# A hybrid RWKV-7 / S5 / RG-LRU layer on one core: gate banks read at another priority, GroupNorm squares one tick sooner, S5 poles fetched at the start, SBUF pools opened in another order

## The chip, the core and the metric

The kernel runs on one core of a Trainium2 chip. A core has a matrix engine (TensorE, in the profile PE, with its weight loads as PEld), a vector engine (VectorE, DVE), an engine for activation functions (ScalarE, ACT), a general engine (GpSimd, POOL) and a queue that issues transfers (SyncE, SP). Each works through its own list of instructions in order, and waits for the others by semaphores. Data lie in SBUF (128 partitions), sums of matmuls in PSUM (8 banks of 128 x 512 float32 here), all else in HBM.

The metric is the device time of one execution in microseconds (us). Before the change it was 1810.94 us, the median of three runs (1809.5 to 1812.85).

## The reference

One layer over a sequence of 2048 positions of width 1024, all float32, then a norm. `linear_binop` joins two steps of a linear recurrence; the helpers that are left out are plain.

```python
def hybrid_layer(h, p_i, norm_g, w_in, ..., w_out, ple_w, ple_norm_g, ple_gate_w):
    zin = rmsnorm(h, norm_g) @ w_in                       # 1024 -> 4224
    z_rw, g_rw, u_s5, g_s5, x_lru, g_lru = jnp.split(zin, SPLITS, axis=-1)
    y_rw = rwkv7_group(z_rw, g_rw, ...)                   # 8 heads of 64
    y_s5 = s5_group(u_s5, g_s5, ...)                      # 32 groups, 64 complex states each
    y_lru = rglru_group(x_lru, g_lru, ...)                # 8 blocks of 64
    h = h + jnp.concatenate([y_rw, y_s5, y_lru], axis=-1) @ w_out
    e = rmsnorm(p_i @ ple_w, ple_norm_g)
    return h + e * jax.nn.sigmoid(h @ ple_gate_w)

# RWKV-7, one step and what follows it
    S = S * d - (S @ kk) b^T + v k^T ;  y = S @ r
    y = (y - mean(y)) * rsqrt(var(y) + RWKV_GN_EPS) * ln_w + ln_b     # GroupNorm by head
    y = (y + sum(r * k * r_k) * v) * silu(gate)

# RG-LRU
    r = sigmoid(xc @ wa + ba) ;  i = sigmoid(xc @ wx + bx)            # blocks of 64
    log_a = -LRU_C * r * softplus(-lam) ;  a = exp(log_a)
    h_t = a_t * h_(t-1) + sqrt(-expm1(2 * log_a)) * (i * xc) ;  y = h * silu(gate)

# S5
    lam = complex(a_re, a_im) ;  lam_bar = exp(lam * dt)              # the poles
    x_t = lam_bar * x_(t-1) + b_bar u ;  y = real(c x) + d u ; then gelu, a gated 512 x 512 product, silu(gate)
```

The outputs of the three groups are gated by their own columns of the input projection.

## The kernel before

**Precision.** A large product is made of three matmuls at float32r: both operands are split into a high and a low part (`whi`, `wlo`, `xh`, `xl`; the high part is a cast on ScalarE, the low part a subtraction on VectorE), and high x high, low x high and high x low are added up in one PSUM bank. So one 128 x 128 weight block and 512 positions cost the three matmuls of L345, L346 and L347 in the input projection, or L949, L950 and L951 in the helper `mm3`.

**First stage: input projection with the RWKV-7 and RG-LRU mixers (to about 1145 us).** The sequence is taken in two halves of 1024, each in two blocks of 512 (`TB`). `fills` yields the input projection column block by column block, and what is done with each: `z` for RWKV, `g` its gates, `l` for RG-LRU, `s` for S5, whose inputs go to HBM for later. Beside the fills run three stages of RWKV, each a generator, over 16 units (two pairs of heads x 256 positions): `front_stage` makes the decayed keys and their products (`kx`, `gr`, `mt`, `bk`), `solve_stage` inverts the triangular systems (`ms`, `xs`, `stmp`, `tm`), `chain_stage` carries the state over four steps of 64 positions, and then norms and gates.

The order on TensorE is written out by hand (`manual_schedule`): a clock of ticks; in each tick the fills issue 10 or 8.8 matmuls' worth (`CHUNK_MM`), and then each stage that is due issues one piece. `yield n` in a stage puts its next piece n ticks later. On the other engines, and on the SP queue, a list scheduler orders the instructions when the kernel is built, by priority (program order less an offset) and by a model of when each is ready. `tc.high_priority` gives the offset: the chain `PR_C` = 100, the solve 50, front and fills 0; `PR_B` = 100 is used for single instructions. After the tick loop TensorE is ordered by the scheduler too.

*RG-LRU gates.* The two gate products of a block are made while a later column block is projected, after its third and fifth group of matmuls (`K_LATE`): `decay_gate` (L686) and `input_gate` (L706) each write a bank of the ring of three that the fills use as well (`ps_mm`). The bank is free for a projection again when ScalarE has read it: twice for the decay gate (`lr` by Abs, `la` by Relu), once for the input gate (`li` by Tanh). The tiles `lr`, `la`, `lth`, `li`, `z`, `xc`, `us`, `g` are buffers of one ring of eight (`tf`).

*GroupNorm of the chain.* A chain's step has three pieces; after the last one of the last step it yields, then ScalarE squares the outputs (`rst` from the bank `ps_y`), it yields again, and L633 sums the squares over the heads into the bank `ps_late`. ScalarE reads that by Ln, and takes Exp for the root. `ps_late` is a single bank, also written by the solve of the next unit (L548, L562). VectorE multiplies, adds the bonus `bon`, multiplies by the gate `g2`, and two transfers store `rst` in HBM (`Yd`).

**Second stage: S5 beside a part of the output projection.** `o1a` makes the product of w_out with the RWKV and RG-LRU outputs, 16 tiles of 128 positions. It needs a tile of `Yd`, loaded as `yr` and split into `yh` and `yl` (`split_y`), and eight rows of w_out, each loaded into a staging buffer `st` and split into `woh` and `wol` (`split_rows`). `yr` and `st` share a ring of three buffers (pool `hq`). The first tile is multiplied row by row, so that it can start with the first row. In the same stretch VectorE works out the S5 parameters from the poles: `a_re` and `a_im` come in by four transfers, two transposes on TensorE (L1035, L1036) turn them, and `ar` and `ai` are copied out.

**Last stages.** The S5 output gate with the rest of w_out, then the per-layer embedding, its gate and the final norm.

**SBUF.** Pools on the right side are stacked from the right edge of SBUF inwards in the order in which they are opened; within a pool, the tag that is asked for first lies at the lowest address, the farthest from the edge. The pools of the first stage on that side, in their order: `rz` (13 KB a partition: `zk`, `zr`, `zl`, `wab`, `pt`, `sp`, `sn`), `rf` (16: the ring `tf`), `re` (8: `bon`, `g2`, `rst`), `rl` (44: `kb`, `gr`, `dl`, `kx`, `tm`, `uv`), `rv` (4: `zv`), `rw` (28: `tp` 12, `bk`, `ms`, small ones, `ep`, `inv`, `mt`, `xs`, `stmp`). They are closed together, and the next stage's pools are stacked from the same edge: `hq` (12: `yr`, `st`, `ht`), `gwp` (16), `wq` (16: `yl`, `yh`), `wpb` (40: five rows of w_out), `wpa` (24: the first three rows). With `reuse_waits="tile"` a new tile waits for the last uses of just those old tiles whose addresses it covers.

Of the kernel before, what the change touches and what calls it, by code (L numbers as in the profile page):

```python
# [17 lines left out]
P = 128  # L18
# [27 lines left out]
def hymba_layer(ctx: ExitStack, tc: tile.TileContext, x, p, norm_g, w_in,  # L46
# [55 lines left out]
    def act(out, in_, func, scale=1.0, bias=0.0):  # L102
        A.activation(out=out, in_=in_, func=func, scale=scale, bias=bias)  # L103
# [17 lines left out]


    rws, xws = ExitStack(), ExitStack()
    rz = rws.enter_context(tc.tile_pool(name="rz", bufs=1, side="right", reuse_waits="tile"))
    rf = rws.enter_context(tc.tile_pool(name="rf", bufs=1, side="right", reuse_waits="tile"))
    re = rws.enter_context(tc.tile_pool(name="re", bufs=1, side="right", reuse_waits="tile"))
    rl = rws.enter_context(tc.tile_pool(name="rl", bufs=1, side="right", reuse_waits="tile"))
    rv = rws.enter_context(tc.tile_pool(name="rv", bufs=1, side="right", reuse_waits="tile"))
    rw = rws.enter_context(tc.tile_pool(name="rw", bufs=1, side="right", reuse_waits="tile"))
    POOL = {"tf": rf, "zk": rz, "zr": rz, "zv": rv, "bon": re, "g2": re, "tc": re}  # L130
    POOL.update((tag, rl) for tag in ("kx", "gr", "tm", "kb", "uv", "dl"))
    POOL.update((tag, rz) for tag in ("pt", "sn", "sp"))
# [167 lines left out]
    V.memset(lru_h, 0.0)  # L300
    s_carry = const.tile([P, 4, 64], F32, name="s_carry")
    V.memset(s_carry, 0.0)


    def lru_rates():
# [263 lines left out]
    def rwkv_chain(pair, half, q, q_, gd):  # L569
# [15 lines left out]
        for st in range(NS):  # L585
# [37 lines left out]
            for c in (st, st + NS):  # L623
                for h, hs in enumerate(heads):
                    T.matmul(out=psy[hs, c * C:(c + 1) * C], lhsT=uv[:, c, h], rhs=gr[:, c, h], start=False, stop=True,
                             tile_position=(0, 64 * h), skip_group_check=True)
            yield 1
        chained.append(0)
        rst = wt("rst")
        act(rst, psy, AF.Square)  # L630
# [48 lines left out]
    def lru(ct, half, xn, b, wg, wab, xc):  # L679
        g2 = gate2(tmp_f("g2"), (yield from inproj(xn, wg, b)))  # L680

        keep = []

        def decay_gate():
            psr = pmm()
            T.matmul(out=psr, lhsT=wab[:, 0], rhs=xc, start=True, stop=True)  # L686
            r_ = tmp_f("lr")
            act(r_, psr, AF.Abs, scale=0.5, bias=dcol(o_ba, ct))
            act(r_, r_, AF.Tanh)
            a = tmp_f("la")  # L690
            act(a, psr, AF.Relu, scale=-1.0, bias=dcol(o_nba, ct))
            act(a, a, AF.Exp, scale=-1.0)

            stt(r_, r_, 1.0, a, ALU.add, ALU.mult)
            th = tmp_f("lth")
            act(th, r_, AF.Tanh, scale=dcol(o_sp, ct))
            act(a, r_, AF.Exp, scale=dcol(o_sm, ct))
            act(r_, a, AF.Square)
            stt(th, r_, 1.0, th, ALU.add, ALU.mult)
            act(th, th, AF.Sqrt, scale=0.25)  # L700
            keep.append((r_, a, th))

        def input_gate():
            r_, a, th = keep[0]
            psi = pmm()
            T.matmul(out=psi, lhsT=wab[:, 1], rhs=xc, start=True, stop=True)  # L706
            ti = tmp_f("li")
            act(ti, psi, AF.Tanh, scale=0.5, bias=dcol(o_bx, ct))
            stt(ti, ti, 1.0, xc, ALU.add, ALU.mult)
            mul(ti, ti, th)  # L710
            h = r_
            V.tensor_tensor_scan(out=h, data0=a, data1=ti, initial=lru_h[:, ct:ct + 1], op0=ALU.mult, op1=ALU.add)
            V.tensor_copy(out=lru_h[:, ct:ct + 1], in_=h[:, TB - 1:TB])
            mul(h, h, g2)
            spill_y(h, Yd, 4 + ct, half * HALF + b * TB)

        late.extend((decay_gate, input_gate))
# [32 lines left out]
    def fills(half, xt, w, prev):  # L750
# [39 lines left out]
        yield from beside(lora(wl, zl, 0, xn), second, 1)  # L790
        yield from beside(rwkv_in(0, 0, zd[0], xn, 0, wk), second, 1)
        yield from second
        yield from lora(wl, zl, 1, xn)
        more()
        yield from rwkv_in(0, 0, zd[0], xn, 1, wk)
        if half == 0:
            lru_rates()

        def both(f, *a):
# [161 lines left out]

    s5c, ow = ExitStack(), ExitStack()
    hq = ctx.enter_context(tc.tile_pool(name="hq", bufs=1, side="right", reuse_waits="tile"))
    gwp = ctx.enter_context(tc.tile_pool(name="gwp", bufs=1, side="right", reuse_waits="tile"))
    wq = ctx.enter_context(tc.tile_pool(name="wq", bufs=1, side="right", reuse_waits="tile"))
    wpb = ow.enter_context(tc.tile_pool(name="wpb", bufs=1, side="right", reuse_waits="tile"))
    wpa = ow.enter_context(tc.tile_pool(name="wpa", bufs=1, side="right", reuse_waits="tile"))
    sc = s5c.enter_context(tc.tile_pool(name="s5c", bufs=1, side="left", reuse_waits="tile"))
# [26 lines left out]
        if i + 2 < NT:  # L995
            o1a_load(i + 2)

    NG = 32
    st32 = sc.tile([NG, 2, P], F32, name="st32")
    for i, src in enumerate((s5_a_re, s5_a_im)):  # L1000
        for h in range(2):
            nc.sync.dma_start(out=st32[:, i, 64 * h:64 * h + 64], in_=src[0])
    first_y = o1a_y(0)
    woh, wol = split_rows(wpa, w_out[0], (0, 1, 2), "wo", stage_q)
    for rows_, more in zip((woh, wol), split_rows(wpb, w_out[0], (3, 8, 9, 10, 11), "wo", stage_q)):
# [10 lines left out]
                o1a(i)  # L1016


    ar = sc.tile([P, NG], F32, name="ar")
    ai = sc.tile([P, NG], F32, name="ai")  # L1020
    al = sc.tile([P, NG], F32, name="al")
    thp = sc.tile([P, NG], F32, name="thp")
    rho = sc.tile([P, NG], F32, name="rho")
# [7 lines left out]
    pid = sc.tile([P, T5, NG], F32, name="pid")  # L1031
    tmps = [sc.tile([P, NG], F32, name=f"stm{i}") for i in range(8)]
    t0_, t1_, t2_, t3_, t4_, t5_, t6_, t7_ = tmps
    ps = pprep()
    T.transpose(out=ps[:, 0:NG], in_=st32[:, 0], identity=ident[0:NG, 0:NG])  # L1035
    T.transpose(out=ps[:, NG:2 * NG], in_=st32[:, 1], identity=ident[0:NG, 0:NG])  # L1036
    V.tensor_copy(out=ar, in_=ps[:, 0:NG])
    V.tensor_copy(out=ai, in_=ps[:, NG:2 * NG])
    nc.sync.dma_start(out=t0_, in_=s5_log_dt.broadcast_to([P, NG]))
    act(t0_, t0_, AF.Exp)  # L1040
    mul(al, ar, t0_)
# [400 lines left out]
```

## Time and profile before

| what | value |
|---|---|
| time, median of 3 runs | 1810.94 us (1809.5 to 1812.85) |
| the profiled execution's own time | 1812.73 us |
| its span, first to last instruction | 1810.8 us |
| mean granted TensorE clock | 0.984 |
| TensorE busy | 1730.4 us (96%) |
| VectorE, ScalarE busy | 1238.9 us (68%), 940.0 us (52%) |
| transfers, mean | 131 GB/s |

The profile gives for each engine what it did, how long, and, where it sat idle before an instruction, what ended that wait, in the form "idle us <- engine, tile, line". Lines are those of the kernel before. Ends of matmuls are modelled, so the pace of TensorE is read from start to start: 0.23 us for a matmul of 128 x 512. The granted clock is the share of its full rate that TensorE was given in a stretch.

### The profile page before, as it was taken

The numbers are of one execution on the slowest core, as the hardware profiler recorded it, in microseconds if no ns is written. First come the engines' busy times: TensorE is split into PE (matmuls) and PEld (weight loads), VectorE is DVE, ScalarE is ACT, GpSimd is POOL, SyncE is SP. The second block draws the span as 40 slices with busy tenths as digits, with TensorE's granted clock in tenths as the row PEclk, the third lists the DMA queues.
The fourth block names the chain that finished last, engine by engine and source line by source line (L and its number), as shares of the span: only waits on it lengthen the run. The fifth ranks groups of instructions, "written<-read, shape, count | busy, mean of one in ns | idle before, by whom it ended". The sixth has DMA issues, their size and how long they took to land. (4 is left out here: it accounts for less than half of the span.)

```text
span 1810.8 us, 30089 instructions
## 1 busy us (share of the span) xinstructions
PE 1730.4 (96%) x11212; PEld 1330.8 (73%) x11212; DVE 1238.9 (68%) x3121; ACT 940.0 (52%) x1792; POOL 43.8 (2%) x105
## 2 busy tenths in 40 slices
PE   5999899989998999999998999799999999999997
PEld 4877677767776777677766667588888778888886
DVE  6268877778897338877777875787866685555554
ACT  5346745575777433745557466475763452222222
POOL 1000000000000000000000000000000000000000
PEclk9999999999999999999999999899999999999999
DMA  5664435433444353234323232733324893222220
GB/s 194 213 202 138 152 108 170 161 104 118 148 134 137 117 178 143 87 106 138 131 82 96 72 96 81 208 123 109 119 89 142 221 310 125 85 104 100 83 68 35
DMA packets 198779, 236.61 MB, mean 131 GB/s; under 512 B 60309, under 2 KB 149738, under 8 KB 198634
## 3 DMA queue, kind: packets, MB, share of 16 engines
q1 hardware_dynamic: 198634, 234.70, 40.3%
q8 instruction: 88, 1.44, 0.3%
q14 instruction: 57, 0.47, 0.1%
HBM read 139.03 MB, written 94.44 MB: 129 GB/s over the span
## 5 line engine op out<-in xcount | busy, mean ns | idle before, releaser
L345 PE MATMUL ps_mm<-xh,whi 128*128 128x512 f32 x1056 | 466.0, 441 | 5.2 <-ACT la L103 5.2
L347 PE MATMUL ps_mm<-xl,whi 128*128 128x512 f32 x1056 | 417.4, 395 | 0.0
L346 PE MATMUL ps_mm<-xh,wlo 128*128 128x512 f32 x1056 | 417.0, 395 | 0.0
L345 PEld LDWEIGHTS ps_mm<-xh,whi 128*128 128x128 f32 x1056 | 200.5, 190 | 83.3 <-issue 32.3
L346 PEld LDWEIGHTS ps_mm<-xh,wlo 128*128 128x128 f32 x1056 | 201.3, 191 | 46.6 <-issue 13.9
L347 PEld LDWEIGHTS ps_mm<-xl,whi 128*128 128x128 f32 x1056 | 200.5, 190 | 45.6
L82 DVE TENSOR_TENSOR xs<-xs,stmp 128x60 f32<-128x60 f32 (+24 forms) x496 | 103.1, 208 | 12.7
L82 DVE TENSOR_TENSOR stmp<-xs,ms 128x60 f32<-128x60 f32 (+24 forms) x496 | 103.4, 209 | 12.1
L949 PE MATMUL ps_mm<-woh,yh 128*128 128x512 f32 x256 | 102.8, 402 | 3.8 <-ACT yh L103 3.8
L950 PE MATMUL ps_mm<-woh,yl 128*128 128x512 f32 x256 | 103.1, 403 | 1.0 <-DVE yl L100 1.0
L951 PE MATMUL ps_mm<-wol,yh 128*128 128x512 f32 x256 | 101.7, 397 | 0.0
L951 PE MATMUL ps_mm<-pgl,hh 128*128 128x512 f32 x256 | 101.1, 395 | 0.3 <-DVE pgl L82 0.3
L950 PE MATMUL ps_mm<-pgh,hl 128*128 128x512 f32 x256 | 100.9, 394 | 0.0
L949 PE MATMUL ps_mm<-pgh,hh 128*128 128x512 f32 x256 | 100.8, 394 | 0.0
L103 ACT ACT_TABLE_LOAD x75 | 96.2, 1283 | 1.3
L100 DVE SCALAR_TENSOR_TENSOR z<-ps_mm,pc,z 128x511 f32<-128x511 f32 x48 | 35.7, 743 | 77.9 <-ACT z L103 77.6
L103 ACT ACTIVATE ftg<-ps_mm 128x512 f32<-128x512 f32 x32 | 19.1, 598 | 134.4 <-PE ps_mm L951 134.4
L100 DVE SCALAR_TENSOR_TENSOR e<-ftg,e 128x1024 f32<-128x1024 f32 x16 | 19.6, 1225 | 77.2 <-ACT ftg L103 77.2
L103 ACT ACTIVATE z<-ps_mm,dc 128x512 f32<-128x512 f32 x48 | 32.9, 686 | 73.9 <-PE ps_mm L347 73.7
L103 ACT ACTIVATE uv<-ps_chain 64x128 f32<-64x128 f32 x64 | 17.4, 272 | 80.6 <-DVE uv L95 60.2
L949 PEld LDWEIGHTS ps_mm<-woh,yh 128*128 128x128 f32 x256 | 48.5, 190 | 14.3 <-ACT yh L103 4.3
L595 ACT COPY sn<-uv 64x128 f32<-64x128 f32 x96 | 28.4, 296 | 58.3 <-DVE uv L82 56.8
(332 smaller groups left out, 3493.0 us busy)
## 6 DMA issues: line engine op xcount, KB each, us to landing
wraw<-in_w_in SPq DMA_DIRECT2D x66, 256.0 KB
Wd<-whi SPq DMA_DIRECT2D x33, 512.0 KB
Wd<-wlo SPq DMA_DIRECT2D x33, 512.0 KB
wlo<-Wd SPq DMA_DIRECT2D x33, 512.0 KB
whi<-Wd SPq DMA_DIRECT2D x33, 512.0 KB
zd<-z SPq DMA_DIRECT2D x48, 256.0 KB
yr<-Yd SPq DMA_DIRECT2D x16, 512.0 KB
Hd<-ht SPq DMA_DIRECT2D x16, 512.0 KB
```

The source lines that it names most:

```text
L82: V.tensor_tensor(out=out, in0=a, in1=b, op=op)
L100: V.scalar_tensor_tensor(out=out, in0=a, scalar=s, in1=b, op0=op0, op1=op1)
L103: A.activation(out=out, in_=in_, func=func, scale=scale, bias=bias)
L345: T.matmul(out=ps, lhsT=hi[:, k], rhs=xh, start=(k == 0), stop=False)
L346: T.matmul(out=ps, lhsT=lo[:, k], rhs=xh, start=False, stop=False)
L347: T.matmul(out=ps, lhsT=hi[:, k], rhs=xl, start=False, stop=(k == KD - 1))
L595: A.copy(out=sn[hs], in_=uv[hs, cs, h])
L949: T.matmul(out=ps, lhsT=a_h[:, k], rhs=b_h[k][:, ns], start=(ends[0] and k == 0), stop=False)
L950: T.matmul(out=ps, lhsT=a_l[:, k], rhs=b_h[k][:, ns], start=False, stop=False)
L951: T.matmul(out=ps, lhsT=a_h[:, k], rhs=b_l[k][:, ns], start=False, stop=(ends[1] and k == nk - 1))
```

## The change

1. In `decay_gate` the two reads of the bank (Abs, Relu) stand together ahead of the Tanh, at the priority offset `PR_B`; in `input_gate` the read by Tanh has that offset too.
2. The chain doesn't yield after the last piece of its last step, so that the squares belong to that tick, and L633 to the next one.
3. The poles are fetched in the first half, after the second block of x has been made ready, into a buffer of the ring `tp`; two transposes and one copy bring them into a constant tile after the first RWKV columns. The second stage no longer loads, transposes or copies them.
4. The first stage's pools on the right side are opened in the order `rw`, `rf`, `rz`, `rv`, `rl`, `re`; in the second stage `wq` comes before `gwp`.

```diff
+    rw = rws.enter_context(tc.tile_pool(name="rw", bufs=1, side="right", reuse_waits="tile"))
+    rf = rws.enter_context(tc.tile_pool(name="rf", bufs=1, side="right", reuse_waits="tile"))
     rz = rws.enter_context(tc.tile_pool(name="rz", bufs=1, side="right", reuse_waits="tile"))
-    rf = rws.enter_context(tc.tile_pool(name="rf", bufs=1, side="right", reuse_waits="tile"))
+    rv = rws.enter_context(tc.tile_pool(name="rv", bufs=1, side="right", reuse_waits="tile"))
+    rl = rws.enter_context(tc.tile_pool(name="rl", bufs=1, side="right", reuse_waits="tile"))
     re = rws.enter_context(tc.tile_pool(name="re", bufs=1, side="right", reuse_waits="tile"))
-    rl = rws.enter_context(tc.tile_pool(name="rl", bufs=1, side="right", reuse_waits="tile"))
-    rv = rws.enter_context(tc.tile_pool(name="rv", bufs=1, side="right", reuse_waits="tile"))
-    rw = rws.enter_context(tc.tile_pool(name="rw", bufs=1, side="right", reuse_waits="tile"))
...
+    NG = 32
+    poles = const.tile([P, 2, NG], F32, name="poles")
+    ar, ai = poles[:, 0], poles[:, 1]
+
+    def pole_rows():
+        t = tmp_p("st32")[0:NG, 0:2 * P].rearrange("g (i p) -> g i p", i=2)
+        for i, src in enumerate((s5_a_re, s5_a_im)):
+            for h in range(2):
+                nc.sync.dma_start(out=t[:, i, 64 * h:64 * h + 64], in_=src[0])
+        return t
+
+    def pole_columns(t):
+        ps = pprep()
+        for i in range(2):
+            T.transpose(out=ps[:, i * NG:(i + 1) * NG], in_=t[:, i], identity=ident[0:NG, 0:NG])
+        V.tensor_copy(out=poles, in_=ps[:, 0:2 * NG].rearrange("p (i g) -> p i g", i=2))
...
-            yield 1
+            if st + 1 < NS:
+                yield 1
         chained.append(0)
         rst = wt("rst")
         act(rst, psy, AF.Square)
...
             r_ = tmp_f("lr")
-            act(r_, psr, AF.Abs, scale=0.5, bias=dcol(o_ba, ct))
+            a = tmp_f("la")
+            with tc.high_priority(offset=PR_B):
+                act(r_, psr, AF.Abs, scale=0.5, bias=dcol(o_ba, ct))
+                act(a, psr, AF.Relu, scale=-1.0, bias=dcol(o_nba, ct))
             act(r_, r_, AF.Tanh)
-            a = tmp_f("la")
-            act(a, psr, AF.Relu, scale=-1.0, bias=dcol(o_nba, ct))
...
             ti = tmp_f("li")
-            act(ti, psi, AF.Tanh, scale=0.5, bias=dcol(o_bx, ct))
+            with tc.high_priority(offset=PR_B):
+                act(ti, psi, AF.Tanh, scale=0.5, bias=dcol(o_bx, ct))
...
         yield from second
+        rows5 = pole_rows() if half == 0 else None
         yield from lora(wl, zl, 1, xn)
         more()
         yield from rwkv_in(0, 0, zd[0], xn, 1, wk)
         if half == 0:
+            pole_columns(rows5)
             lru_rates()
...
     hq = ctx.enter_context(tc.tile_pool(name="hq", bufs=1, side="right", reuse_waits="tile"))
+    wq = ctx.enter_context(tc.tile_pool(name="wq", bufs=1, side="right", reuse_waits="tile"))
     gwp = ctx.enter_context(tc.tile_pool(name="gwp", bufs=1, side="right", reuse_waits="tile"))
-    wq = ctx.enter_context(tc.tile_pool(name="wq", bufs=1, side="right", reuse_waits="tile"))
...
-    st32 = sc.tile([NG, 2, P], F32, name="st32")
-    for i, src in enumerate((s5_a_re, s5_a_im)):
-        for h in range(2):
-            nc.sync.dma_start(out=st32[:, i, 64 * h:64 * h + 64], in_=src[0])
...
-    ps = pprep()
-    T.transpose(out=ps[:, 0:NG], in_=st32[:, 0], identity=ident[0:NG, 0:NG])
-    T.transpose(out=ps[:, NG:2 * NG], in_=st32[:, 1], identity=ident[0:NG, 0:NG])
-    V.tensor_copy(out=ar, in_=ps[:, 0:NG])
-    V.tensor_copy(out=ai, in_=ps[:, NG:2 * NG])
```

More of the change, by code (lines that the diff above doesn't have):

```diff
@@ L996, in o1a @@
             o1a_load(i + 2)
-    NG = 32
-    st32 = sc.tile([NG, 2, P], F32, name="st32")
-    for i, src in enumerate((s5_a_re, s5_a_im)):
-        for h in range(2):
-            nc.sync.dma_start(out=st32[:, i, 64 * h:64 * h + 64], in_=src[0])
     first_y = o1a_y(0)
@@ L1016, in o1a_next @@
                 o1a(i)
-    ar = sc.tile([P, NG], F32, name="ar")
-    ai = sc.tile([P, NG], F32, name="ai")
     al = sc.tile([P, NG], F32, name="al")
```

## The prediction

> **What bounds the kernel now.** I read the page's busy times first, then the waits of TensorE (PE) in the mixers' stretch, then granted clocks by stretch, then the timeline around the stage change and around the waits.
>
> ```profile
> PE 1730.4 (96%) x11212; PEld 1330.8 (73%) x11212; DVE 1238.9 (68%) x3121; ACT 940.0 (52%) x1792; POOL 43.8 (2%) x105
> ```
>
> PE sets the time: it is busy for 96% of the span, and the change adds and removes no matmul that counts. What can change is the rest: PE's waits, and the time that it runs at half clock behind them. The waits from 150 to 1145 us (waiter, what it waited for: us in total, times, longest):
>
> ```profile
> PE ps_chain L614 <- ACT uv L103: 6.6, 10, 1.1
> PE ps_mm L345 <- ACT la L103: 5.2, 2, 3.0
> PE ps_late L548 <- ACT rst L103: 5.1, 4, 2.1
> PE ps_prep L476 <- DVE bk L82: 3.6, 1, 3.6
> ...
> PE ps_late L548 <- DVE stmp L508: 3.5, 1, 3.5
> PE ps_mm L686 <- ACT li L103: 3.3, 1, 3.3
> ```
>
> Some waits are followed by a stretch at half clock. The column after the engines' busy times is the granted clock:
>
> ```profile
> 219.00:229.25 10.25, 10.02 (x94) 7.98 (x95) 4.32 (x11) 4.81 (x13) 0.61 (x2) 0.50 0.37 115
> 393.10:396.50 3.40, 2.85 (x5) 1.61 (x6) 2.58 (x4) 2.70 (x6) 0.00 (x0) 0.50 0.16 45
> 771.95:775.40 3.45, 3.45 (x32) 2.33 (x32) 2.06 (x4) 2.66 (x7) 0.00 (x0) 0.51 0.38 128
> 1055.30:1058.70 3.40, 3.40 (x9) 2.31 (x8) 0.80 (x2) 2.88 (x6) 0.00 (x0) 0.50 0.27 77
> 1145.05:1153.03 7.98, 0.57 (x2) 0.35 (x2) 6.43 (x16) 5.35 (x7) 0.00 (x0) 0.65 0.80 239
> 1153.03:1157.65 4.62, 4.40 (x10) 3.04 (x11) 2.89 (x6) 1.36 (x3) 0.00 (x0) 0.50 0.87 291
> ```
>
> A stretch with busy PE at 0.50 loses half of its busy time: 5.0, 1.4, 1.7, 1.7 us, and 2.2 us for the last row.
>
> **The stage change (pools, poles).** TensorE, then ScalarE, VectorE and the SP queue:
>
> ```profile
> 1144.43 0.39 PE L346 MATMUL ps_mm<-xh,wlo 128*128 128x512 f32 x1
> 1144.66 0.39 PE L347 MATMUL ps_mm<-xl,whi 128*128 128x512 f32 x1
> 1148.57 0.28 PE L1035 MATMUL ps_prep<-ident,st 32*128 32x32 f32 x1 [3.52 <-DMA st<-in_s_a_re]
> 1153.03 1.22 PE L949 MATMUL ps_mm<-woh,yh 128*128 128x512 f32 x2 [3.78 <-ACT yh L103]
> 1155.06 0.63 PE L951 MATMUL ps_mm<-wol,yh 128*128 128x512 f32 x1
> ```
> ```profile
> 1141.94 1.05 ACT L107 CAST woh<-st 128x1024 fp32r<-128x1024 f32 x1 [0.64 <-DMA st<-in_w_out]
> ...
> 1144.31 0.63 ACT L103 ACTIVATE rst<-rst 128x512 f32<-128x512 f32 x1
> 1150.98 1.04 ACT L107 CAST woh<-st 128x1024 fp32r<-128x1024 f32 x1 [1.90 <-DMA st<-in_w_out]
> 1151.93 1.05 ACT L103 ACTIVATE yh<-yr 128x1024 fp32r<-128x1024 f32 x1
> ...
> 1163.06 1.04 ACT L107 CAST woh<-st 128x1024 fp32r<-128x1024 f32 x1
> ```
> ```profile
> 1135.44 0.29 DVE L82 TENSOR_TENSOR s_carry<-sp,dl 128x128 f32<-128x128 f32 x1
> ...
> 1147.89 0.69 DVE L82 TENSOR_TENSOR rst<-rst,g 128x512 f32<-128x512 f32 x1
> 1156.10 1.23 DVE L82 TENSOR_TENSOR wol<-st,woh 128x1024 fp32r<-128x1024 f32 x1 [1.69 <-ACT woh L107]
> ```
> ```profile
> 1136.22 0.43 SPq L106 DMA_DIRECT2D st<-in_w_out  x1
> 1139.90 4.71 SPq L106 DMA_DIRECT2D st<-in_w_out  x2
> 1144.66 0.89 SPq L1002 DMA_DIRECT2D st<-in_s_a_re  x2
> 1148.65 0.90 SPq L369 DMA_DIRECT2D Yd<-rst  x2
> ```
>
> The last input projection ends at 1145.05, and PE does nothing of weight until 1153.03. First it waits for the poles, whose fetch stands in SP's queue behind a row of w_out that waits for its buffer (4.71 us). Then it waits for `yh`, which stands in ScalarE's queue behind a cast that waits for its row.
>
> By the pools' sizes in the code (KB counted from the right edge): before, `rz` takes 13, then `rf` 16, `re` 8, `rl` 44, `rv` 4, `rw` 28. The next stage's `hq` (0 to 12: yr and the staging rows) lies on the chain's `pt`, `sp`, `sn` and on `zl`, `zk`, `zr`; `yh` (28 to 44 holds `wq`) lies on `bon` and `g2`, which the last GroupNorm reads at 1147.89. After, `rw` is at the edge: `hq` lies on `stmp`, `xs`, `mt`, `ep`, `ms` and `wq` on `bk` and `tp`, all of front and solve, done before the last chain starts. So yr and two rows can be fetched long before 1136.22, and `yh` needs only its cast. What is late next: `wpa` (84 to 108) now lies on `kx`, `gr`, `kb` (free with the chain's last step, which `s_carry` ends at 1135.73) and its outermost tile, `wol0`, on `rst` itself. So the first L951 waits for the last store of `rst` to land, then for a subtraction of 1.23.
>
> I take the store's end to come 3 us earlier than now: 2 from one tick of GroupNorm (below), and 1 because no `woh` cast that waits for its row stands ahead of Exp (1141.94: 0.64 and part of 1.05). Now it is issued from 1148.65 to 1149.55; with 2 us to land (an estimate between 0.9, its issue alone, and 5.7, the first row from 1136.22 to its cast at 1141.94) it ends at 1151.6, then at 1148.6; plus 1.2: L951 at about 1149.8 against 1155.06, a gain of 5.2. The rows must keep up: the eight come now from 1136.22 to 1163.06, one in 3.4 us. Three can be there by 1145; the other five end at 1162 at that pace, at 1156.4 if a cast and a subtraction (1.04 + 1.23) are the pace; the middle, 1159, is 4 sooner than now. Behind the shorter gap half of the 2.2 of clock stays. I take **-5**; bounds 0 (rows pace it as now) and -10.2 (7.98 and 2.2 all gone). The poles' four issues (0.89 for two, so 1.8 us of SP) and two transposes go to the start, behind the second x block, where the first fills hide them: **+0.5**, bounds 0 and +2 (the full issue stands ahead of a weight load that PE needs).
>
> **The gate banks.** The waits named `la` and `li`, with the ScalarE instructions that end them:
>
> ```profile
> 393.65 2.07 PE L686 MATMUL ps_mm<-xc,wab 128*128 128x512 f32 x2 [3.33 <-ACT li L103]
> 403.90 0.50 PE L345 MATMUL ps_mm<-xh,whi 128*128 128x512 f32 x1 [2.21 <-ACT la L103]
> 1053.50 0.50 PE L345 MATMUL ps_mm<-xh,whi 128*128 128x512 f32 x1 [3.00 <-ACT la L103]
> ```
> ```profile
> 392.92 0.69 ACT L103 ACTIVATE li<-ps_mm,dc 128x512 f32<-128x512 f32 x1
> 1052.76 0.69 ACT L103 ACTIVATE la<-ps_mm,dc 128x512 f32<-128x512 f32 x1 [0.76 <-DVE li L82]
> ```
>
> `li` read its bank behind Ln, Exp and two table loads; read first, it costs PE nothing, and the gap of 3.33 goes with its 1.4 of clock. `la` is another matter: at 1052.76 ScalarE was idle and waited for VectorE's `li`, which frees the `tf` buffer that `la` needs (8 buffers). A higher priority doesn't free it; it only pulls the other block's `li` and Relu forward, so that its decay is done sooner. So 3.33 + 1.4 = 4.7, and half of 2.21 + 3.00 + 1.7 = 3.5; 2.2 of it I take off again, because PE, earlier after 393.65, meets the wait at 403.90 earlier too. **-6**; bounds 0 and -11.6 (3.33 + 2.21 + 3.00 + 1.4 + 1.7).
>
> **The squares.** `rst` is squared in the chain's last tick, so the L633 matmul comes one tick sooner: 10 or 8.8 projections of 0.23 us (1144.43 to 1144.66), so 2.3 or 2.0 us.
>
> ```profile
> 219.23 1.06 PE L548 MATMUL ps_late<-stmp,mt 32*32 32x32 f32 x32 [3.51 <-DVE stmp L508]
> ...
> 770.59 0.69 PE L548 MATMUL ps_late<-stmp,mt 32*32 32x32 f32 x32 [2.13 <-ACT rst L103]
> ```
> ```profile
> 218.04 0.69 DVE L82 TENSOR_TENSOR rst<-ps_y,rst 128x512 f32<-128x512 f32 x1 [0.87 <-ACT rst L103]
> 218.65 0.43 DVE L508 STREAM_TRANSPOSE stmp<-xs 128x256 f32<-128x256 f32 x1
> ```
> ```profile
> 972.88 0.60 ACT L103 ACTIVATE rst<-ps_y 128x512 f32<-128x512 f32 x1
> ```
>
> L548 writes the bank that Ln must have read; 2.0 us sooner covers the 2.13 at 770.59 and its 1.7 of clock. At 219.23 the transposition stood on VectorE behind `rst`, which waited 0.87 for ScalarE: 0.87 of 3.51 is sure to go, and with a shorter gap perhaps a quarter of the 5.0 of clock, 1.3. The other L548 waits (5.1 - 2.13 = 3.0) stand just ahead of the `bk` wait of 3.6, where ScalarE and VectorE are late themselves, so I give them 0.5. Against it: the square now has one tick to end before L633; at 972.88 it ran late, which costs about 0.5. Sum 2.1 + 1.7 + 0.9 + 1.3 + 0.5 - 0.5 = **-6**; bounds +1 and -15.3 (5.1 + 3.5 + 5.0 + 1.7). Chain, solve and front keep their ticks, since a chain starts when its solve is done, not when the one before has ended.
>
> [...]
>
> **Order on ScalarE.** 48 gate reads of 0.69 us (16 each of Abs, Relu, Tanh) now stand level with the chain's `uv` copies, for which PE already waits ten times. I take **+2** (three full reads, 2.07, in the way); bounds 0 and 33 (all).
>
> **Sum.** -5 + 0.5 - 6 - 6 + 2 = -14.5. The profiled execution took 1812.73 (span 1810.8 and 1.9 around it): 1798.2. It stands 1.8 above the median of the runs, 1810.94, so the median to expect is 1796.4.
>
> **The rivals.**
>
> *The waits only move* (0.25): PE meets `bk` (3.6), the ring of `tf` and the late chain a little earlier and waits there; gates and squares give a third, -4: -5 + 0.5 - 4 + 2 = -6.5, so 1804.4. For it: 1052.76 waits for a buffer and not for its turn. Against it: nothing stands behind the 2.13 at 770.59.
>
> *The clock stays up* (0.15): the gaps at 219, 393, 770 and 1053 fall under what starts the half rate: stage change -8, gates -9, squares -11, +0.5: -27.5, so 1783.4. Against it: each needs VectorE on time too.
>
> *Nothing comes* (0.05): the rows of w_out pace the stage change and ScalarE's order in the mixers falls out as before: about 1810.
>
> *Gate reads ahead of the chain's copies* (0.05): each of the 48 that lands just ahead of a `uv` copy holds L614 for 0.69. From 24 of them (16.5 us) the gain is eaten; with 32, 22 - 16.5 = +5.5: 1816. For it: L614's ten waits of up to 1.1. Against it: the gates' matmuls lie between the chain's steps, and ScalarE is busy for 52% only.
>
> **How the numbers follow.** Forecast 0.5, with its own range 1790 to 1802. Two in ten outside: the lower half of the clock case, "nothing", and the slow one; so 1784 to 1808. A measurement tells about 0.2% (3.6 us) from no change: below 1807.3 lie the forecast, the clock case and 0.22 of the moving waits: faster 0.87; same 0.08 (0.03 + 0.05), slower 0.05.
>
> **What would show it.** Right: no wait of PE for a pole; `yh` cast before 1145; PE's gap at the stage change about 4 us and ended by `wol`; no L686 wait for `li`; L548 waits for `rst` near nothing; PEclk near 1 at 393 and 771. Wrong: L345 waits for `la` as long as now or longer, L614's waits doubled, `woh` casts that still come 3.4 us apart until 1163, or new waits of L633 for the square.

## The result, and the profile after

The changed kernel takes 1825.22 us (median of 4 runs, 1821.69 to 1825.87), the kernel before beside it 1811.68 (1809.5 to 1812.85): a ratio of 1.0072, 95% interval 1.0055 to 1.009. It is slower, where a gain of 14.5 us was forecast. Its profiled execution is the fastest of its runs, 1821.69 with a span of 1820.0, 9.2 longer than the span before.

The page's busy times, then the waits of TensorE from 150 to 1145 us (waiter, what it waited for: us in total, times, longest):

```profile
PE 1734.0 (95%) x11212; PEld 1333.5 (73%) x11212; DVE 1238.9 (68%) x3120; ACT 940.7 (52%) x1792; POOL 43.8 (2%) x105
...
PE ps_late L580 <- DVE tm L530: 7.8, 3, 3.3
PE ps_chain L632 <- ACT uv L103: 6.8, 10, 1.1
PE ps_prep L350 <- DVE xl L100: 5.2, 3, 3.6
PE ps_late L580 <- ACT stmp L572: 4.2, 5, 2.2
PE ps_mm L705 <- ACT li L103: 4.1, 1, 4.1
PE ps_prep L494 <- DVE bk L82: 2.9, 2, 2.3
PE ps_mm L363 <- DMA whi<-Wd: 2.4, 1, 2.4
PE ps_mm L363 <- ACT la L103: 2.1, 1, 2.1
```

Lines are from here on those of the kernel that is read: in the changed one L345 of the kernel before is L363, L548 is L566, L562 is L580, L949 is L972. The work is the same, 11212 matmuls, but TensorE is busy 3.6 us longer with it: its mean granted clock is 0.981 in place of 0.984. The waits have other names: those for `rst` are gone, but L580, the next instruction of the solve on the same bank, now waits 7.8 us for `tm` and 4.2 for `stmp`. The wait for `li` is still there, and longer.

To find the place of the loss I compared the start of the same matmul of 128 x 512, counted from the first, in the two profiles. After less before:

| stretch of the kernel before | at its start | at its end |
|---|---|---|
| 155 to 557 us | 0.0 | -4.5 |
| 557 to 604 (last blocks of the first half, first of the second) | -4.5 | +1.1 |
| 604 to 1115 | +1.1 | +1.5 |
| 1115 to 1209 (the stage change) | +1.5 | +8.0 |
| 1209 to the end | +8.0 | +9.2 |

So 4.5 us were won, 5.6 given back within 47 us, and 6.5 lost at the stage change. There, TensorE, ScalarE, VectorE and SP:

```profile
1153.17 1.22 PE L972 MATMUL ps_mm<-woh,yh 128*128 128x512 f32 x2 [6.66 <-ACT yh L103]
```
```profile
1147.04 1.98 ACT L107 CAST woh<-st 128x1024 fp32r<-128x1024 f32 x2
1151.27 0.23 ACT L103 ACTIVATE stm<-stm 128x32 f32<-128x32 f32 x1 [2.25 <-DMA stm<-in_s_log_dt]
1151.94 0.23 ACT L103 ACTIVATE stm<-al 128x32 f32<-128x32 f32 x1 [0.44 <-DVE al L82]
1152.08 1.04 ACT L103 ACTIVATE yh<-yr 128x1024 fp32r<-128x1024 f32 x1
...
1157.44 1.04 ACT L107 CAST woh<-st 128x1024 fp32r<-128x1024 f32 x1 [1.75 <-DMA st<-in_w_out]
...
1169.05 1.05 ACT L107 CAST woh<-st 128x1024 fp32r<-128x1024 f32 x1 [0.85 <-DMA st<-in_w_out]
```
```profile
1149.44 2.36 DVE L82 TENSOR_TENSOR wol<-st,woh 128x1024 fp32r<-128x1024 f32 x2 [1.50 <-DMA Yd<-rst]
```
```profile
1102.74 0.88 SPq L106 DMA_DIRECT2D st<-in_w_out  x2
...
1147.01 0.88 SPq L387 DMA_DIRECT2D Yd<-rst  x2
1147.94 0.49 SPq L1050 DMA_DIRECT2D stm<-in_s_log_dt  x1
...
1152.74 2.35 SPq L106 DMA_DIRECT2D st<-in_w_out  x3
...
1155.80 5.53 SPq L1124 DMA_DIRECT2D b<-in_s_b_re  x1
```

No pole is waited for, and two rows are fetched at 1102.74 already. But their staging buffers are free only when `wol` is made, which waits for the store of `rst` until 1149.44; the third row comes 10 us after the first two, and the last is cast at 1169.05 (before: 1163.06). `yh` stands behind the exponential of `log_dt`, whose fetch is queued behind that store.

### The profile page after: what moved, and what is told of

It is laid out like the page before. It is cut to its first block, busy times and chain, and to the rows that moved or that the text cites. A ratio compares the mean times of both kernels' runs of the same rounds, so it can differ in the third digit from the quotient of the medians.

```text
span 1820.0 us, 30068 instructions
## 1 busy us (share of the span) xinstructions
PE 1734.0 (95%) x11212; PEld 1333.5 (73%) x11212; DVE 1238.9 (68%) x3120; ACT 940.7 (52%) x1792; POOL 43.8 (2%) x105
## 5 line engine op out<-in xcount | busy, mean ns | idle before, releaser
L363 PE MATMUL ps_mm<-xh,whi 128*128 128x512 f32 x1056 | 465.5, 441 | 4.5 <-DMA whi<-Wd 2.4
L363 PEld LDWEIGHTS ps_mm<-xh,whi 128*128 128x128 f32 x1056 | 201.0, 190 | 82.9 <-issue 32.6
L364 PEld LDWEIGHTS ps_mm<-xh,wlo 128*128 128x128 f32 x1056 | 201.6, 191 | 46.3 <-issue 13.7
L972 PE MATMUL ps_mm<-woh,yh 128*128 128x512 f32 x256 | 105.5, 413 | 9.1 <-ACT yh L103 6.7
L82 DVE TENSOR_TENSOR xs<-xs,stmp 128x60 f32<-128x60 f32 (+24 forms) x496 | 103.3, 208 | 12.9
L972 PE MATMUL ps_mm<-pgh,hh 128*128 128x512 f32 x256 | 100.8, 394 | 0.0
L972 PEld LDWEIGHTS ps_mm<-woh,yh 128*128 128x128 f32 x256 | 49.6, 194 | 20.8 <-ACT yh L103 7.1
L103 ACT ACTIVATE uv<-ps_chain 64x128 f32<-64x128 f32 x64 | 17.5, 273 | 82.0 <-DVE uv L95 63.1
```

Source lines behind the costliest of these rows:

```text
L82: V.tensor_tensor(out=out, in0=a, in1=b, op=op)
L363: T.matmul(out=ps, lhsT=hi[:, k], rhs=xh, start=(k == 0), stop=False)
L364: T.matmul(out=ps, lhsT=lo[:, k], rhs=xh, start=False, stop=False)
L972: T.matmul(out=ps, lhsT=a_h[:, k], rhs=b_h[k][:, ns], start=(ends[0] and k == 0), stop=False)
```

## The experiments

Each was timed in three rounds beside the kernel before, whose medians were 1811.03 to 1812.05. The runs of one kernel lie up to 6.5 us from their median, and the profiled one can be an outer one: it is 6.5 us below the median in after_no_sq, 5.5 in after_bq, 3.5 in after_re and in the changed kernel, 3.0 in sq_low, and 5.2 us above it in only_poles, 3.0 in pools_re. So a profile is read here for its places, and times are compared by the medians and ratios.

| kernel | median us | ratio to before (95%) |
|---|---|---|
| only_pools | 1814.45 | 1.0028 (1.0014 to 1.0042) |
| only_poles | 1812.76 | 1.0017 (1.0004 to 1.003) |
| only_gates | 1810.98 | 1.0003 (0.9994 to 1.0013) |
| only_squares | 1813.92 | 1.0016 (1.0004 to 1.0028) |
| after_no_sq | 1817.80 | 1.0026 (1.0014 to 1.0038) |
| low_only | 1811.14 | 0.9996 (0.9986 to 1.0005) |
| sq_low | 1806.70 | 0.9971 (0.9959 to 0.9982) |
| sq_low_gates | 1811.75 | 0.9996 (0.9985 to 1.0006) |
| after_re | 1814.67 | 1.0020 (1.0007 to 1.0033) |
| stage_only | 1815.16 | 1.0022 (1.0012 to 1.0032) |
| all_mended | 1812.81 | 1.0005 (0.9996 to 1.0014) |
| pools_re | 1814.78 | 1.0016 (1.0007 to 1.0025) |
| after_bq | 1817.61 | 1.0027 (1.0016 to 1.0038) |
| pools_re_bq | 1809.30 | 0.9988 (0.9977 to 0.9999) |
| before_bq | 1816.03 | 1.0028 (1.0016 to 1.0040) |
| sq_low_bq | 1808.50 | 0.9988 (0.9979 to 0.9998) |
| sq_low_stage_bq | 1805.76 | 0.9957 (0.9941 to 0.9972) |
| sq_low_pools_bq | 1804.26 | 0.9952 (0.9933 to 0.9971) |

**The four parts, each alone.** The edits are the four parts of the change, each on the kernel before; of each, what tells it (of the pools, the new order by name):

```diff
# only_pools: the new order of both stages' pools
+    rw, rf, rz, rv, rl, re          # first stage, from the edge
+    hq, wq, gwp                     # second stage
# only_poles
+        rows5 = pole_rows() if half == 0 else None
+            pole_columns(rows5)
# only_gates: Abs and Relu together, and Tanh of li, under
+            with tc.high_priority(offset=PR_B):
# only_squares
-            yield 1
+            if st + 1 < NS:
+                yield 1
```

> The kernel before with the pools alone in the new order (both stages); nothing else changed. Theory A (addresses: wol0 lies on rst, so the staging buffers of the first rows are held until the store of rst has landed, and the later rows come behind it): the mixers up to 1116 us keep their times within 1 us, the last rows of w_out are cast some 6 us later than 1163.06, TensorE has new waits for woh behind the first tile, and the time is 4 to 9 us above the kernel before (1816 to 1821). Theory B (queues: without the poles' fetch and with the transfer of log_dt behind the stores, SP and ScalarE come to another order; the addresses are harmless): rows and yh come no later than now, TensorE's gap behind 1145.05 is 4 to 8 us, and the time is 0 to 6 us below.

> The kernel before with the poles alone fetched and turned early; pools, gates and squares as before. Theory A: harmless, the wait of 3.52 us for the poles goes or its time is waited for yh instead; the time is 0 to 4 us below the kernel before. Theory B: yh comes behind the exponential of log_dt on ScalarE, as in the changed kernel, the rows come later, and a good part of the loss behind 1145 us is here: 3 to 8 us above.

> The kernel before with the gate banks alone read first, at the higher priority. Theory C (the mixers' loss around the half boundary at 557 to 604 us, 5.6 us in the changed kernel, comes from the gate reads in ScalarE's order): a loss of 2 to 6 us appears there in this kernel, and it comes out 0 to 6 us above the kernel before. Theory D (it comes from the squares): offsets stay within 1 us through that stretch, the waits for li and la go or stay as they are, and the time is between 5 us below and equal.

> The kernel before with the squares alone in the chain's last tick. Theory C: the gains of some 1.9 us at 221 us and of 1 to 3 us at 390 to 557 us are here and nothing is lost at the half boundary; 2 to 5 us below the kernel before. Theory D: the same early gains, then the 5.6 us lost at 557 to 604 us and the waits for tm at 222 and 776 us (the solve's bank reached by an earlier Ln, with VectorE not earlier): within 1 us of the kernel before or up to 4 us above.

None of them gains; pools, poles and squares each lose. The product of the four ratios is 1.0064, near the 1.0072 of the whole. Where each loses, by the same count of matmuls: the pools from 1115 to 1209 (-1.3 to +3.3, Theory A), the poles there too (-0.4 to +5.3, though `yh` is not late by `log_dt` there). That the poles are not harmless rests on the ratio; how much they cost is open, since this profile is of an outer run. The squares lose from 557 to 604 (-5.1 to +0.9) and another 2.9 at 772 to 790 (Theory D). The gates lose nothing (Theory C falls).

Why the gates gain nothing, from ScalarE and TensorE, first before, then with the gates alone:

```profile
385.34 0.59 ACT L103 ACTIVATE km<-ta,dc 128x256 f32<-128x256 f32 x1
```
```profile
386.82 0.67 ACT L103 ACTIVATE li<-ps_mm,dc 128x512 f32<-128x512 f32 x1
...
396.37 0.58 ACT L103 ACTIVATE km<-ta,dc 128x256 f32<-128x256 f32 x1
...
398.93 2.79 PE L476 MATMUL ps_prep<-kx,bk 64*128 64x128 f32 x16 [4.76 <-DVE bk L82]
```

`li` is read 6 us sooner and its wait of 3.33 is gone. But `km` of the front, at priority 0, is put 11 us back, VectorE needs it for `bk`, and TensorE now waits 4.76 for `bk` five us further on.

**The squares: who is late in their place.** VectorE before, VectorE and TensorE after:

```profile
770.28 0.45 DVE L512 STREAM_TRANSPOSE tm<-stmp 128x256 f32<-128x256 f32 x1
771.01 0.44 DVE L512 STREAM_TRANSPOSE tm<-stmp 128x256 f32<-128x256 f32 x1
...
772.78 0.69 DVE L82 TENSOR_TENSOR rst<-ps_y,rst 128x512 f32<-128x512 f32 x1 [0.88 <-ACT rst L103]
```
```profile
771.99 0.69 DVE L82 TENSOR_TENSOR rst<-ps_y,rst 128x512 f32<-128x512 f32 x1 [0.88 <-ACT rst L103]
...
774.00 0.64 DVE L82 TENSOR_TENSOR rst<-rst,bon 128x512 f32<-128x512 f32 x1
...
774.89 0.68 DVE L82 TENSOR_TENSOR rst<-rst,g 128x512 f32<-128x512 f32 x1
775.49 0.43 DVE L530 STREAM_TRANSPOSE tm<-stmp 128x256 f32<-128x256 f32 x1
```
```profile
776.08 0.69 PE L580 MATMUL ps_late<-tm,stmp 32*32 32x32 f32 x32 [3.34 <-DVE tm L530]
```

GroupNorm has the chain's priority, 100; the solve has 50, the input's splits 0. Ready one tick sooner, its products stand ahead of the transposition of `tm` that TensorE needs next. To test that, GroupNorm behind its sum was put 100 lower:

```diff
# sq_low: only_squares, and
+        with tc.high_priority(offset=-100):
             act(rst, psr, AF.Ln, scale=1.0 / 64, bias=gneps)
             ...                    # Exp, products, gains, stores
# low_only: the same without the earlier squares
# sq_low_gates: sq_low with the gates of the change
```

> The kernel with the squares alone early, and everything of the GroupNorm behind its sum (Ln, Exp, products, stores) at a priority 100 lower. Theory V (GroupNorm, at the chain's priority, now comes ready sooner and passes the solve's copies and transpositions and the input's splits on ScalarE and VectorE): the wait for tm at 776 us (4.1 us) falls below 1, the loss of 6.0 us at 557 to 604 shrinks to below 3, and the time is 3 to 8 us below that of the squares alone: 1806 to 1811. Theory W (the earlier matmul itself, not the order on the other engines): both losses stay and the time is within 2 us of the squares alone, 1812 to 1816.

> The kernel before with the GroupNorm behind its sum at a priority 100 lower, the squares where they were. Theory V (the order on ScalarE and VectorE is what counts, not the tick of the squares): most of the 5 us gained by the squares at low priority comes without the squares, 1805 to 1809. Rival (the earlier tick is needed, as the later Ln would hold the solve's bank still longer): the waits for rst of 5.1 us grow, and the time is 1811 to 1818.

> The squares early, the GroupNorm low, and the gate banks read first. If the gate reads have a worth once the GroupNorm is out of their way (the waits for li, 1.6 and 0.8, and for la, 3.4 and 2.1, that the kernel without them still has), 2 to 5 us below it: 1802 to 1805. If they only move, as alone (1810.98 against 1811.05): within 1.5 us of 1806.7.

sq_low gains 0.29%, 5.2 us below the kernel before by the ratio: Theory V. Its VectorE and TensorE:

```profile
771.58 0.44 DVE L512 STREAM_TRANSPOSE tm<-stmp 128x256 f32<-128x256 f32 x1
...
774.08 0.69 DVE L82 TENSOR_TENSOR rst<-rst,bon 128x512 f32<-128x512 f32 x1 [1.20 <-ACT rst L103]
```
```profile
772.18 0.69 PE L562 MATMUL ps_late<-tm,stmp 32*32 32x32 f32 x32 [1.45 <-ACT stmp L554]
```

`tm` comes ahead of the `bon` sum; the wait is 1.45 where only_squares had 3.93, and the unit at 772 to 790 us costs 5.0 less. From 557 to 604 it loses 0.7 instead of 6.0, but most of that is only moved: at 512 TensorE waits for VectorE's `xsv`, behind `rst` all the same, and goes to half clock, 5.5 lost where only_squares lost 1.1:

```profile
512.80 0.97 PE L562 MATMUL ps_late<-tm,stmp 32*32 32x32 f32 x32 [2.42 <-DVE xsv L82]
```

From 604 to 1110 us it gains 9.3, where only_squares gains 1.6. The lower priority alone does nothing (low_only): the earlier tick is needed, but pays only where its followers do not push in. With the gates on top the gain is gone (sq_low_gates, 5 us above sq_low). Here too `bk` is waited for, 3.33 at 397.34, but by 557 the two profiles are level again (-1.3 and -1.1 against the kernel before). What sq_low wins and sq_low_gates doesn't lies at 772 to 790 (3.9 us) and at 1050 to 1060 (3.7): L562 waits 2.29 for `rst` where sq_low has 1.45 for `stmp`, L345 waits 2.82 for `la` where sq_low has 1.93, and with each come 6.8 us at half clock that sq_low hasn't got. TensorE of sq_low_gates:

```profile
774.23 1.06 PE L562 MATMUL ps_late<-tm,stmp 32*32 32x32 f32 x32 [2.29 <-ACT rst L103]
```

Why `rst` is late there was not followed further.

**The squares left out of the whole.** after_no_sq is the changed kernel with `yield 1` put back.

```diff
-            if st + 1 < NS:
-                yield 1
+            yield 1
```

> The changed kernel with the squares put back where they were: pools, poles and gates alone. If the parts simply add up (5.1 for the pools, 3.1 for the poles, 0.5 for the gates, 2.9 for the squares by their ratios), it takes 1819 to 1821, 3 us below the changed kernel's ratio, the 5.6 us lost at 557 to 604 are gone and the loss at 1153 to 1209 stays. If the loss at the stage change comes from the squares (the earlier GroupNorm), the time is 1812 to 1816.

The 5.6 us at 557 to 604 are gone (-3.3 to -2.8 there), the stage change loses as much as before (5.5 from its first product with w_out to 1181), and the time, 1817.8, lies between the two numbers expected. The parts do not add up exactly: taking the squares out of the whole gives 7.4 us, and alone they cost 2.9.

**The stage change: where rst lies.** `re` (with `rst`) is opened third in place of last; `wol0` then lies on `rl`, and `rst` under the last row.

```diff
# after_re: the changed kernel; stage_only: before + poles + pools; pools_re: before + pools
     rw
     rf
+    re
     rz
     rv
     rl
-    re
# all_mended: after_re, and GroupNorm low as in sq_low
```

> The changed kernel with one pool moved: re (bon, g2, rst) is opened third instead of last, so that wol0 and woh0 lie on rl, and rst under the last row of w_out. Theory A (addresses: wol0 on rst holds the staging buffers): the first rows are cast before Ln of the last GroupNorm, some 6 to 8 us sooner than 1147.04; the last row is cast at 1160 to 1163 instead of 1169.05, the waits for woh go, and of the 7.7 us lost between 1116 and 1209 us at least 4 come back: 1816 to 1821. Theory B (ScalarE's and SP's order): yh still stands behind the exponential of log_dt, TensorE still starts at 1152 to 1153 and its gap of 6.7 us stays; the time stays within 2 us of the changed kernel's.

> The kernel before with the stage change alone: the poles early, and the pools in the order of the changed kernel but for re, which is opened third; gates and squares as before. Theory A: the rows are cast early and nothing waits for them; the stage change gives what the prediction gave it, 2 to 6 us below the kernel before. Theory B: without the pole transposes TensorE stands still until yh, which ScalarE casts behind the exponential of log_dt: the gap is 6 to 8 us long and followed by half clock, and the time is 0 to 6 us above the kernel before.

> The changed kernel with both mends: re opened third, and the GroupNorm behind its sum at a priority 100 lower. If the two causes found so far (addresses at the stage change; GroupNorm ahead of the solve and the splits on ScalarE and VectorE) are all there is, the mixers end some 10 us sooner than in the kernel before, as with the squares at low priority, and the stage change costs 1 to 3 us more than before, as in the two kernels with re third: 1801 to 1806. If the parts disturb each other (gates against the later GroupNorm on ScalarE), 1807 to 1814.

> The kernel before with the pools alone in the new order, but re third. Theory A: against the pools in the order of the changed kernel (1814.45, a loss of 7.8 us from the first product with w_out to 1181) the rows come 6 us sooner and the loss behind the first product is below 3; 3 to 6 us below that kernel: 1808 to 1811. Rival (the loss is the order of queues that comes with any move of hq and wq): 1813 to 1816 again.

after_re takes back 9.4 of the 13.0 us (1.0072 to 1.0020). About half of that is the stage change, by the table below; the rest lies before 1115 us, where the two differ in addresses alone: the wait for `whi` is missing, and so are 6.8 us at half clock, which in the changed kernel come with a wait of 2.15 us for `la` (at 1054.55) that after_re has as well. Whether they would be there in another execution was not tried. Its ScalarE:

```profile
1130.77 1.99 ACT L107 CAST woh<-st 128x1024 fp32r<-128x1024 f32 x2
...
1145.23 0.23 ACT L103 ACTIVATE stm<-stm 128x32 f32<-128x32 f32 x1 [0.93 <-DMA stm<-in_s_log_dt]
1145.37 1.04 ACT L103 ACTIVATE yh<-yr 128x1024 fp32r<-128x1024 f32 x1
...
1156.21 1.05 ACT L107 CAST woh<-st 128x1024 fp32r<-128x1024 f32 x1 [1.58 <-DMA st<-in_w_out]
```

So that stage changes at different times can be compared, each is counted from the end of its own last input projection (worked out from the timelines):

| kernel | first product with w_out | last row cast | 193rd product |
|---|---|---|---|
| before | 8.1 | 18.2 | 64.3 |
| changed | 6.8 | 22.7 | 70.9 |
| only_pools | 4.7 | 23.5 | 69.0 |
| only_poles | 8.4 | 19.1 | 70.0 |
| after_re | 6.4 | 16.2 | 65.8 |
| pools_re | 3.6 | 17.5 | 69.3 |
| after_bq | 12.9 | 25.0 | 68.4 |
| pools_re_bq | 3.8 | 17.3 | 64.5 |
| before_bq | 11.1 | 20.8 | 69.7 |
| sq_low_pools_bq | 10.4 | 17.4 | 64.0 |

The address decides the rows: with `wol0` on `rst` the last one is cast at 22.7 to 25.0, with `re` third at 16.2 to 17.5. That part of Theory A holds. Of Theory B the gap holds too: in after_re the wait for `yh` is still 6.28 us, and stage_only, which came out at 1815.16 as its Theory B had it, casts `yh` behind the exponentials and has a gap of 7.48. all_mended, at 1812.81, missed the 1801 to 1806 that it would have taken if the two causes were all: it has the waits of sq_low_gates, 2.30 for `rst` and 2.8 for `la`, so the gates disturb the low GroupNorm there too.

And pools_re, with its rows in time, is no faster than only_pools: here the expectation missed. At the 96th product it is still 2.1 us ahead of only_pools, at the 193rd it is 0.3 behind. SP and TensorE of pools_re:

```profile
1157.59 4.64 SPq L1113 DMA_DIRECT2D b<-in_s_b_re  x1
1162.34 1.34 SPq L955 DMA_DIRECT2D yr<-Yd  x1
```
```profile
1170.90 0.79 PE L950 MATMUL ps_mm<-woh,yl 128*128 128x512 f32 x1 [1.14 <-DVE yl L100]
1199.90 1.96 PE L1195 MATMUL ps_prep<-q,z 128*128 128x16 f32 x16 [1.12 <-ACT kin L103]
```

The transfers of S5's `b` hold up the queue, and `yr` of the second tile is issued behind them; TensorE waits for `c` (1.14, to 1167.60), for that `yl` and then for `kin`, and runs at half clock from 1168.2 to 1175.1 and from 1202.4 to 1205.8.

**S5's b off the SP queue.** Its four transfers were issued from GpSimd.

```diff
# *_bq
-        nc.sync.dma_start(out=dst[0:64], in_=a)
-        nc.sync.dma_start(out=dst[64:128], in_=b)
+        G.dma_start(out=dst[0:64], in_=a)
+        G.dma_start(out=dst[64:128], in_=b)
# after_bq, pools_re_bq, before_bq: on the kernel of that name
# sq_low_bq: on sq_low; sq_low_pools_bq: and the pools with re third; sq_low_stage_bq: and the poles
```

> The changed kernel with the four transfers of S5's b issued from GpSimd's queue instead of SP's; addresses as in the changed kernel (wol0 on rst). Theory Q (the queue: b ahead of rows 3 and on): the last row is cast some 4 to 6 us before 1169.05, the waits for woh at 1162.7 and 1166.7 go, and 3 to 6 us of the loss come back: 1819 to 1822. Theory A (the address alone): the rows come as late as now, within 1.5 us of 1825.

> The kernel before with the new pools, re third, and b from GpSimd's queue. Theory Q: rows 9 to 11 come 3 to 5 us sooner than at 1159.8 to 1163.1, the second stretch at half clock (1168 to 1175) goes, and the stage change gives a gain at last: 1806 to 1811. If c's transfers take b's place in front of the rows: 1812 to 1815.

> The kernel before with nothing changed but S5's b from GpSimd's queue. If that mends only the order that the new pools brought (in the kernel before, b is issued from 1157.74 on, behind the last row): within 2 us of 1811.7. If it is a gain of its own: 1805 to 1809, and the 5 us of the pools with b off the queue are not theirs.

> Squares early, GroupNorm low, b from GpSimd's queue; pools and poles as before. If the new pools add something once b is out of the way: 1806 to 1808, 2 to 3 us above the same with the pools (1804.26). If they add nothing: 1803 to 1805.

> The same with the poles left at the stage change, where yh is cast ahead of the exponential of log_dt. If yh is what counts there: 1800 to 1805, 1 to 4 us below the kernel with the poles early. If the poles' wait (5.2 and 1.6 us with the squares early) counts instead: 1805 to 1810.

> Squares early with the GroupNorm low, the poles early, the pools with re third, b from GpSimd's queue, gates as before. If the gains add (4.8 of the low GroupNorm, 0 to 4 of the mended stage change): 1802 to 1807. If yh, cast behind the exponential of log_dt, sets the end of TensorE's gap whatever the rows do: 1807 to 1811.

after_bq is 7.6 us below the changed kernel, but not by the reason I gave: its rows come no sooner. From the store of `rst` to the last cast it takes 24.4 us, in the changed kernel 22.0 (1147.01 to 1169.05):

```profile
1143.68 0.87 SPq L387 DMA_DIRECT2D Yd<-rst  x2
```
```profile
1168.08 1.05 ACT L107 CAST woh<-st 128x1024 fp32r<-128x1024 f32 x1 [1.24 <-DMA st<-in_w_out]
```

What changes at the stage change is TensorE's waits. The changed kernel from 1140 to 1215 us, then after_bq from 1137 to 1212:

```profile
PE ps_mm L972 <- ACT yh L103: 6.7, 1, 6.7
PE ps_mm L972 <- ACT woh L107: 2.4, 2, 1.7
PE ps_prep L1206 <- ACT kin L103: 1.0, 1, 1.0
```
```profile
PE ps_prep L1146 <- DMA cst__12759<-in_s_c_im: 12.2, 2, 9.0
```

With b gone from SP, `c` (the tile `cst`) comes earlier and is transposed in the gap; TensorE starts its products later, waits for hardly any row (0.7 in all for `wol`), and has one long gap in place of three waits with half clock behind each (10.2, 6.8 and 3.4 us, against 13.7 once). By the table that is worth 2.5 us (70.9 to 68.4). The two profiles are 9.6 us apart, and 3.3 of that lie before 1115 us, ahead of any transfer that was moved, where the changed kernel's profile happens to have more half clock (eleven times 3.4 us against eight). So most of the 7.6 is not accounted for. With `re` third, b off the queue gives 5.5 us (1814.78 to 1809.30): the second `yh` is cast 19.5 us from the fills' end instead of 21.6, and the waits for its `yl` and for `kin` are gone but for 0.2. The control, before_bq, is slower by 0.28%: there b is in flight from 1140 on, at the same time as the rows. ScalarE and TensorE of before_bq:

```profile
1149.14 1.04 ACT L107 CAST woh<-st 128x1024 fp32r<-128x1024 f32 x1 [4.85 <-DMA st<-in_w_out]
```
```profile
1151.19 1.22 PE L949 MATMUL ps_mm<-woh,yh 128*128 128x512 f32 x2 [6.36 <-ACT yh L103]
```

So with b out of the way the pools gain beside their control: pools_re_bq is 6.7 us below before_bq, and sq_low_pools_bq 4.2 below sq_low_bq, with intervals that don't meet. But moving b alone had made the controls slower (before_bq clearly, sq_low_bq by 1.8 us against sq_low), so a part of that gain only takes back this loss. Against the same kernels with b on SP it is less, 2.2 (0.9988, an interval that ends just below 1) and 2.4 (1806.70 to 1804.26, not clear of the noise). sq_low_pools_bq, at 0.9952 (4 runs), is the fastest measured, faster than both kernels, though its interval meets sq_low's; the poles early add nothing to it (1805.76).

## Why the prediction was wrong, point by point

**Pools and poles at the stage change, forecast -5.** The step that failed is "the rows must keep up": its bounds ran from 1156.4 to the present 1163.06, and the last row was cast at 1169.05. I saw that `wol0` lies on `rst`, and let that delay one product. It delays a ring: the subtraction that waits for the store is also what frees the staging buffer, so the rows behind it wait too. Right were the wait for the poles that goes, the two rows fetched early (1102.74), and the landing of the store (estimated 2 us after its issue; by 1149.44, 1.6 us after the issue ended at 1147.89). "`yh` needs only its cast" failed too: it was cast at 1152.08, not before 1145, since the scheduler's order on ScalarE and not its data sets it. With `re` and `b` moved the pools are worth 4 to 7 us beside the same kernel with `b` moved, and about 2, hardly clear of the noise, beside the one without.

**Poles at the start, forecast +0.5.** Right for the start: 0.0 at 155 us in only_poles. The loss, 3.1 us by the ratio (0.7 to 5.4), is at the other end. I took the pole transposes away from a gap that `yh` ends anyway: first product at 8.4 instead of 8.1, but the gap is now one piece of 8.22 us where it was 3.52 and 3.78, and behind the first product half clock lasts 7.8 us (1152.88 to about 1160.7, by the starts of the matmuls) where it was 4.6 (1153.03 to 1157.65); the second `yh` is later too. This account is argued from one run, 5.2 us slower than the median of its kernel. TensorE of only_poles:

```profile
1152.88 1.22 PE L969 MATMUL ps_mm<-woh,yh 128*128 128x512 f32 x2 [8.22 <-ACT yh L103]
```

**Gate banks, forecast -6, and ScalarE's order, +2.** Measured 0. The wait for `li` was rightly read (gone in only_gates) and that for `la` too (2.8 us are left of it in only_gates, since a buffer is what it needs). What failed is where the price of the order was looked for: not the chain's `uv` copies, whose waits hardly moved (6.6 to 7.2), but `km` of the front. In the whole change not even `li` got its turn (4.1): GroupNorm, now sooner, stood ahead of it.

**Squares, forecast -6.** "Chain, solve and front keep their ticks" is true of TensorE only. VectorE and ScalarE took GroupNorm first, at its priority, and L580 waited for `tm` instead of L548 for `rst`; at the half boundary the same order held up `xl`, and SP's store of `rst` stood ahead of a weight load (the wait of 2.4 for `whi`). That the store causes that wait is not shown: after_re has the same order there and no such wait. Worth of the step alone: +2.9. With the right order behind it: -5.

**The rivals.** "The waits only move" described the mixers, to the sign: I gave it a third of the gain, and it took all. The slower case was priced on `uv` copies, where nothing happened. No rival let pools, poles and squares each lose by itself. That the sum took the four edits as independent is not what failed: their ratios multiply to 1.0064, near the whole. In the mended kernels it doesn't hold, since the gates take away what the low GroupNorm gives.

## What to carry to other kernels

An instruction that comes ready sooner and has a high priority pushes its whole tail ahead of others on in-order engines; when you move a step, list what stands behind it in each queue, and give the tail the priority that its own users need. An address that is reused late costs not one wait but the pace of the ring whose buffers it holds, so lay under the first-needed tile something that has long been dead. Time each part alone and in pairs: here three of four lost and none gained; the squares gained once their tail stood lower, and the pools showed theirs only with a transfer moved that they don't touch.

## What was not expected of the hardware

The stretches at half clock were 3.4, 6.8, 10.2 or 13.7 us long in the profiles read here, and waits of nearly one length came with different ones. Granted clock behind the first solve's wait, and that wait, in only_pools and then in low_only (the column after the busy times is the clock):

```profile
220.05 0.76 PE L548 MATMUL ps_late<-stmp,mt 32*32 32x32 f32 x32 [3.56 <-DVE stmp L508]
220.50:223.90 3.40, 3.40 (x23) 2.66 (x18) 1.81 (x4) 1.10 (x4) 0.61 (x2) 0.50 0.27 68
```
```profile
219.39 1.06 PE L548 MATMUL ps_late<-stmp,mt 32*32 32x32 f32 x32 [3.50 <-DVE stmp L508]
218.10:224.95 6.85, 5.56 (x57) 4.20 (x59) 4.16 (x8) 2.96 (x7) 0.61 (x2) 0.50 0.50 146
```

In the profile before it was 10.25 us, with a wait of 3.51. So waits of 3.50 to 3.56 us came with 3.40, 6.85 and 10.25 us at half clock. Shorter waits came with half clock or without. In the profile before, the wait of 2.13 at 770.59 was followed by 3.45 us at 0.51 (771.95 to 775.40); after the wait of 2.21 at 403.90 the granted clock was 1.00 until 410.72. The amount changes with the execution too: in 31 runs of the kernel before, timed beside low_only, the mean granted clock was 0.981 to 0.988. What decides whether a stretch comes, and how long it is, was not shown.

Half of TensorE's busy time in the three stretches at the first solve is 1.7, 2.8 and 5.0 us (3.40, 5.56 and 10.02 busy at 0.50; an estimate). So the 1.3 us that I gave to a shorter stretch there could not be forecast from its wait.

The other: a row of w_out issued at 1142.32 was cast at 1149.14 in before_bq, 6.8 us, beside b's four transfers of 128 KB; in the kernel before the same row took 3.7 us (1147.29 to 1150.98). That b's transfers are the cause is argued from their time alone.
